# First norm of a two-layer attention trunk: half of the row tiles squared from a second load of x; another matmul price for the planner

## The chip, the cores and the metric

The kernel runs on one core of a Trainium2 chip. The metric is the time of one execution on the device in microseconds (us), as the median of several runs. Profiles show one execution: TensorE (PE, its weight loads PEld), VectorE (DVE), ScalarE (ACT), GpSimd (POOL) and SyncE (SP), which issues all DMAs here.

## The reference

The trunk has two layers, each x <- x + W_out(mixer(RMSNorm(x)) * silu(gate)), with x of 1024 rows by 1024 columns in float32. Layer A is a sliding-window attention (window 128, 16 query heads, 2 key heads, a sink per head). Layer B is a dilated attention with three groups of heads whose results are merged by their softmax denominators. One input projection gives queries, keys, values and the gate. The part that the change touches is the norm ahead of layer A (its mixer gets h = rmsnorm(x, norm_a)):

```python
def rmsnorm(x, g):
    xf = x.astype(jnp.float32)
    y = xf * jax.lax.rsqrt(jnp.mean(xf * xf, axis=-1, keepdims=True) + EPS)
    return (y * g.astype(jnp.float32)).astype(x.dtype)

def mixer_a(h, w_in, q_gain, k_gain, sinks, cos, sin):
    z = h @ w_in
    q, k, v, gate = jnp.split(z, [nq, nq + nk, nq + 2 * nk], axis=-1)
    ...
    return o.reshape(b, s, BRANCH_WIDTH) * jax.nn.silu(gate)
```

## The kernel before

**Tiles and numbers.** The 1024 rows are 8 row tiles of 128 (t = 0 to 7), the 1024 input columns 8 blocks of 128 (k). Each float32 operand of a matmul is split into a rounded high part (fp32r, made by a copy on ScalarE) and a low part (the difference, on VectorE); each product is three matmuls: high with high, high with low, low with high (`mm3`). So a projection of one row tile is 8 x 3 = 24 matmuls (`proj_tile`, tiles `psz`).

**The front.** The input holds x twice: as it is, and as `xt`, in which each row tile is laid out transposed, with the columns of x on the partitions. `load_xt` (tiles `xt`, three buffers, two DMAs for each tile) loads it, `split` makes `hT` from it, the first operand of the projection. The gain of the norm is multiplied into the weights when they are split (`load_w`: loads `raw` or, for half of the first block, `wbig`; splits `wt`). The factor 1 / rms of each row comes in after the matmuls, as the scale with which ScalarE copies the result `psz` out of PSUM into `z`. For that factor, line 761 on, each row tile's x is squared in its transposed layout (`sqx`, on GpSimd since `SQ` is 0), summed over the blocks k by VectorE (`sr`, 128 x 1024 to 128 x 128), transposed by TensorE (`pr`), summed over what is then the free dimension by VectorE (`nss`), and raised to the power -1/2 by GpSimd (`rstd`, into `ra`). `proj_tile` has two PSUM buffers, so the matmuls of tile t + 2 wait until ScalarE has copied out tile t, and so for `ra` of tile t. `z` goes to DRAM and is fetched again for the attention (`bounce`, `fetch`).

**The rest.** Layer A runs four such blocks of heads, with gate blocks (`psg`) and output products (`psw`) between them; layer B twelve (four blocks of heads, three groups each). A unit of attention (128 in all) is: transposes of queries and keys (`pq`), scores (`pss`), a scaled maximum on VectorE, exponentials on ScalarE (`pe`), transposes (`ptt`), the product with the values (`po`), and a merge of heads. Projections and output products are independent of it, and are set between its steps on TensorE. `norm_scale` is the second norm's square, on ScalarE with a running sum (`hn`).

**What sets the order.** Class `Plan` records all instructions in program order and then issues them by a list scheduler. Each instruction has a price in ns (`_cost`), and each pair of engines a latency. At each step the engine that is free first takes, of the instructions whose operands are there, the one with the lowest number, which is its place in program order minus a bias. So the order on every engine, SP included, follows from the prices; on the chip each engine keeps to that order and waits where an operand isn't there. The price of a DMA is its size at 300 bytes per ns, behind the DMAs issued before it, plus fixed times. Buffers of one tag are used in turn (a ring): the instruction that first writes a buffer waits for the last user of its former content.

Of the kernel before, what the change touches and what calls it, by code (L numbers as in the profile page):

```python
# [12 lines left out]
F32 = mybir.dt.float32  # L13
F32R = mybir.dt.float32r
AF = mybir.ActivationFunctionType
OP = mybir.AluOpType
AX = mybir.AxisListType.X

P = 128
D = 1024  # L20
T = 1024
NT = T // P
NK = D // P
# [10 lines left out]
SQ = 0  # L34
# [19 lines left out]
NB = {"pz": 2, "pS": 2, "pT": 2, "pO": 1, "pM": 1}  # L54
# [40 lines left out]


class Plan:
    """Records the instructions in program order, then issues them engine by engine in the order
    that a list scheduler finds: of the instructions whose operands are there, the earliest in
    program order first, so that the projections fill what the attention leaves of TensorE."""  # L100

    ENGINES = ("PE", "ACT", "DVE", "POOL", "SP")
    LAT = {("PE", "PE"): 0, ("PE", "ACT"): 200, ("PE", "DVE"): 200, ("PE", "POOL"): 200, ("PE", "SP"): 200,
# [141 lines left out]
def _cost(eng, name, out, ins):  # L245
    n = out.free_size()
    if eng == "PE":
        if name == "transpose":
            return 109
        return 213 if n < 2 * P else n / 2.4 + 3  # L250
    if eng == "SP":
        return out.size() * 4 / 300.0
    if eng == "DVE":
        if name == "tensor_reduce":
            n = ins[0].free_size()
        if name == "reciprocal":
            return 60 + 6.5 * n
        if name == "tensor_scalar":
            return 130 + 0.53 * n
        return (140 if name in ("tensor_tensor_reduce", "scalar_tensor_tensor") else 70) + 1.04 * n  # L260
    if eng == "ACT":
        return (60 if len(ins) == 1 else 160) + 0.84 * n
    return 150 + 2.1 * n
# [27 lines left out]
def trunk(ctx, tc, x, norm_a, w_in_a, q_gain_a, k_gain_a, sinks_a, w_out_a,  # L291
          norm_b, w_in_b, q_gain_b, k_gain_b, w_out_b, xt, const, out):
    nc = Plan(tc)
    x, out = x[0], out[0]
# [4 lines left out]
    def pool(name, bufs=1, **kw):  # L299
        return ctx.enter_context(tc.tile_pool(name=name, bufs=bufs, **kw))  # L300

    cp = pool("const")
    sp = pool("work")
# [5 lines left out]
    pM = pool("pm", NB["pM"], space=PS)  # L309
# [1 line left out]
    def f(ap):  # L311
        return ap.bitcast(F32)

# [1 line left out]
    ident = nc.tile(cp, [P, P], F32, name="ident")  # L315
    make_identity(tc.nc, ident)
    con = nc.tile(cp, [P, CS_W + 6 * P], F32, name="con")
# [10 lines left out]
    def load_xt(t):  # L328
        a = nc.tile(sp, [P, NK, P], F32, tag="y", bufs=3, name="xt")
        for k in range(0, NK, 4):  # L330
            nc.sync.dma_start(a[:, k:k + 4], xt[t][:, k:k + 4])
        return a
# [35 lines left out]
    x1d = tc.dram_tile([T, D], F32, name="x1d")  # L368
    xpd = tc.dram_tile([T, D], F32, name="xpd")

# [1 line left out]
    def split(hi, lo, src, g=None, sub=nc.vector):  # L372
        if g is None:
            nc.scalar.activation(hi, src, AF.Copy)
            sub.tensor_tensor(lo, src, f(hi), op=OP.subtract)
        else:
            nc.scalar.activation(hi, src, AF.Copy, scale=g)
            nc.vector.scalar_tensor_tensor(lo, src, g, f(hi), op0=OP.mult, op1=OP.subtract)
# [25 lines left out]
    def rstd(dst, ss, mul, add):  # L404
        nc.gpsimd.tensor_scalar(dst, ss, mul, add, op0=OP.mult, op1=OP.add)
        nc.gpsimd.tensor_tensor(dst, dst, ex[:, :dst.shape[1]], op=OP.pow)

    def alloc_h(j):
        return [nc.tile(sp, [P, NK, 2 * P], F32R, tag=f"h{i}{j}", bufs=1, name="hT") for i in range(2)]
# [243 lines left out]
            nc.sync.dma_start(zi[sl, :width], view(zd))  # L653
        return zi

    # ================= layer A =================
    hT = [alloc_h(j) for j in range(4)]
    hB = {}

    def w_a(n, big=None):  # L660
        return load_w(w_in_a, (0, 384, 640, 1024)[n], 256 if n % 2 else 384, 0, big=big)
# [85 lines left out]
    for n in range(4):  # L747
        w = w_a(n, None if n else nc.tile(sp, [P, 4, 512], F32, tag="v0", bufs=1, name="wbig"))
        if n % 2 == 0:
            ak = nc.tile(sp, [P, 2, NT, P], F32R, tag="v0", bufs=1, name="akr")  # L750
            kv = [ak, nc.tile(sp, [P, NT, P], F32R, tag="v2", bufs=1, name="akv")]
        width = 384 if n % 2 == 0 else 256
        if n == 0:
            zd = tc.dram_tile([T, width], F32, name="za0")
            for t in range(NT):
                nc.bias = FRONT if t < FT else 0
                xr = load_xt(t) if t else xt0
                for k in range(0, NK, 4):
                    split(*(a[:, k:k + 4, t % 2 * P:(t % 2 + 1) * P] for a in hT[t // 2]), xr[:, k:k + 4])
                nc.bias = 0  # L760
                sq = nc.tile(sp, [P, NK, P], F32, tag="p", bufs=2, name="sqx")
                if t < SQ:
                    nc.scalar.activation(sq, xr, AF.Square)
                else:
                    nc.gpsimd.tensor_tensor(sq, xr, xr, op=OP.mult)
                sr = nc.tile(sp, [P, P], F32, tag="zi", bufs=3, name="sr")
                nc.vector.tensor_reduce(sr, sq.rearrange("p k t -> p t k"), axis=AX, op=OP.add)
                pr = nc.tile(pM, [P, 4, P], F32, tag="m", bufs=NB["pM"], name="pr")
                nc.tensor.transpose(pr[:, 0], sr, ident)
                ss = nc.tile(sp, [P, 1], F32, tag="nss", bufs=2, name="nss")  # L770
                nc.vector.tensor_reduce(ss, pr[:, 0], axis=AX, op=OP.add)
                rstd(ra[:, t:t + 1], ss, 1.0 / D, EPS)
                if t == LC:
                    late_constants()
                z = proj_tile(hT, t, w, width, ra)
                nc.sync.dma_start(zd[t * P:(t + 1) * P], z[:, :width])
            pr = nc.tile(pM, [P, 4, P], F32, tag="m", bufs=NB["pM"], name="pr")
            nc.tensor.transpose(pr[:NT, 0], ra, ident)
            rr = nc.tile(sp, [NT, P], F32, tag="zi", bufs=3, name="rr")
            nc.vector.tensor_copy(rr, pr[:NT, 0])  # L780
            rd = tc.dram_tile([1, T], F32, name="rd")
            nc.sync.dma_start(rd.rearrange("a (t p) -> (a t) p", p=P), rr)
            rb = [nc.tile(sp, [P, 512], F32, tag="o0", bufs=2, name="rb") for _ in range(2)]
            for i in range(2):
                nc.sync.dma_start(rb[i], rd[:, i * 512:(i + 1) * 512].to_broadcast([P, 512]))
            oa = nc.tile(sp, [P, 4, 2, 2 * P], F32, tag="v1", bufs=1, name="oa")
        else:
            zd = bounce(hT, w, width, f"za{n}", ra)
        wg = load_w(w_in_a, 1280 + n * 256, 256, 0)
        g = gate_block(hT, wg, rb)  # L790
        if n == 3:
            nc.bias = WOA
            y = load_y(0, 0, range(4), sub=YA)
            load_wout_a(range(4), wo, WOA)
            for t in range(6):
                out_a_first(t, None if t else y)
                if t == KA:
                    load_wout_a(range(4, NK), wo, 0)
        for t in range(NT):
            if n == 3 and t in (4, 6):  # L800
                out_a(t - 4)
                out_a(t - 3)
            if t % 2 == 0:
                o = oa[:, t // 2]
                rc = nc.tile(sp, [P, 4, 2], F32, tag="rc", bufs=2, name="rc")
            z = fetch(zd, width, [(slice(0, P), lambda a: a[t * P:(t + 1) * P])])
            qs, r = prep(0, 0, t, z, 5 if n % 2 == 0 else 4, kv if n % 2 == 0 else None, t)
            sk = nsink[:, 4 * n:4 * n + 4]
            nm = nc.tile(sp, [P, 4], F32, tag="nm", bufs=2, name="nm")
            l = nc.tile(sp, [P, 4], F32, tag="l", bufs=2, name="l")  # L810
            slots = [t - 1, t] if t else [0]
            mask = mask_a[:, P:3 * P] if t else mask_a[:, :P]
            tsl = slice(t % 2 * P, (t % 2 + 1) * P)
            attend(qs, r, kv, slots, mask, nm, l, sk,
                   [(o[:HD, :, tsl], slice(0, P))], [(o[HD:, :, tsl], slice(0, P))])
            e = nc.tile(sp, [P, 4], F32, tag="e", bufs=2, name="e")
            nc.vector.tensor_tensor(e, nm, sk, op=OP.subtract)
            nc.scalar.activation(e, e, AF.Exp)
            nc.vector.tensor_tensor(l, l, e, op=OP.add)
            nc.vector.reciprocal(rc[:, :, t % 2], l)  # L820
            if t % 2:
                late.append(partial(merge, 0, n, t // 2, rc[:, None], 1, [o], g))
# [5 lines left out]
    w0 = out_a_whole((6, 7))  # L828
    hT = hB

    # ================= layer B =================
    kk = nc.tile(sp, [P, 2, 4, P], F32R, tag="v2", bufs=1, name="kring")
    kring = [kk, nc.tile(sp, [P, 4, P], F32R, name="vring")]
    ucount = [0]
# [162 lines left out]
```

## Time and profile before

| | |
|---|---|
| time, median of 3 runs | 1298.51 us (1296.77 to 1298.76) |
| span of the profiled execution | 1295.1 us |
| instructions | 25655 |
| moved by DMA | 149.74 MB |

The span runs from the first to the last instruction of one execution and leaves out what lies around it. In the rows further down, an order of time names the start, the length (of several merged instructions together), the engine, the line, the operation, output <- inputs by tile names, sizes, and in brackets the idle time of the engine just before and whom it waited for. As nearly every instruction is recorded by one helper, all have line 286, and tiles tell them apart. The busy time of a matmul includes its way through the array, so that matmuls in a run overlap, and the spacing of a run is shorter than the mean of one.

### The profile page before, as it was taken

The page shows a single profiled execution, that of the slowest core. Times are in us where ns is not written, and L with a number is a line of the kernel's source. Part 1 is how long each engine was busy: PE and PEld are TensorE (multiplying, and loading weights), DVE is VectorE, ACT ScalarE, POOL GpSimd, SP SyncE. Part 2 cuts the span into 40 slices and gives each one's busy share as a digit, 9 for nine tenths or more (in the row PEclk, how much of TensorE's full clock was granted, in tenths as well). Part 3 has the DMA queues.
Part 4 walks back from the last instruction along what each step waited for, and adds up shares of the span by engine and source line. Part 5 has one row for each costly group of instructions (what it writes and reads, how often), then busy time and mean ns, then how long its engine had stood idle before and what let it go on. Part 6 is the DMA issues. An engine that isn't in the chain of part 4 may idle for free. (4 is left out here: it accounts for less than half of the span.)

```text
span 1295.1 us, 25655 instructions
## 1 busy us (share of the span) xinstructions
PE 1257.3 (97%) x7851; PEld 1132.2 (87%) x7851; DVE 1032.6 (80%) x2968; ACT 867.9 (67%) x2365; POOL 703.6 (54%) x1388
## 2 busy tenths in 40 slices
PE   6999999999999999999999999999999999999998
PEld 5999999998778999988889988889988888887777
DVE  8778778777965338778888888988778888779995
ACT  4376766767653347877757877767877767887760
POOL 4764455446410046555577656577556566587621
PEclk9999999999999999999999999999999999999999
DMA  7423223346254133223334323334223344354544
GB/s 242 128 76 110 77 85 102 91 161 185 83 166 142 66 112 100 82 62 105 117 112 128 88 74 94 107 106 137 82 69 106 98 124 133 117 156 135 165 141 157
DMA packets 142666, 149.74 MB, mean 116 GB/s; under 512 B 33576, under 2 KB 129344, under 8 KB 142528
## 3 DMA queue, kind: packets, MB, share of 16 engines
q1 hardware_dynamic: 142528, 148.09, 37.3%
q8 instruction: 63, 1.03, 0.3%
q14 instruction: 75, 0.61, 0.2%
HBM read 105.57 MB, written 42.47 MB: 114 GB/s over the span
## 5 line engine op out<-in xcount | busy, mean ns | idle before, releaser
L286 PE MATMUL psz<-wt,hT 128*128 128x384 f32 (+1 forms) x3072 | 640.9, 344 | 6.1 <-ACT wt L286 3.9
L286 PEld LDWEIGHTS psz<-wt,hT 128*128 128x128 f32 x3072 | 512.9, 191 | 14.8 <-ACT wt L286 4.0
L286 PE MATMUL psg<-hT,wt 128*128 128x256 f32 x1536 | 226.0, 291 | 0.0
L286 ACT ACTIVATE pe<-pe,st 128x128 f32<-128x128 f32 (+1 forms) x384 | 169.5, 443 | 59.8 <-DVE st L286 57.4
L286 PEld LDWEIGHTS psg<-hT,wt 128*128 128x128 f32 x1536 | 203.9, 192 | 2.7
L286 PE MATMUL ptt<-ident,pe 128*128 128x128 f32 x800 | 177.3, 281 | 6.2 <-ACT pe L286 5.4
L286 DVE SCALAR_TENSOR_TENSOR qs<-pq,gt,qs 64x256 fp32r<-64x256 f32 x256 | 123.8, 484 | 42.4 <-ACT qs L286 36.0
L286 POOL TENSOR_TENSOR r<-r,ex 128x5 f32<-128x5 f32 (+1 forms) x128 | 152.8, 1194 | 5.9
L286 ACT ACTIVATE qs<-pq,gt 64x256 fp32r<-64x256 f32 x256 | 120.1, 469 | 46.2 <-PE pq L286 41.0
L286 DVE TENSOR_TENSOR pp<-ptt,pp 128x512 fp32r<-128x512 f32 x200 | 131.7, 685 | 20.9 <-ACT pp L286 18.1
L286 POOL TENSOR_TENSOR sq<-zi 128x320 f32<-128x320 f32 (+1 forms) x128 | 93.4, 730 | 88.0 <-DMA zi<-zb 41.1
L286 PEld LDWEIGHTS ptt<-ident,pe 128*128 128x128 f32 x800 | 104.6, 140 | 39.8 <-ACT pe L286 23.6
L286 DVE CUSTOM_DVE_ANT_0 pe<-pss,con,r 128x256 f32<-128x256 f32 x288 | 127.7, 476 | 10.5 <-PE pss L286 8.7
L286 ACT ACTIVATE oh<-po 64x512 f32<-64x512 f32 x128 | 76.1, 595 | 81.3 <-PE po L286 79.8
L286 DVE SCALAR_TENSOR_TENSOR wt<-raw,gt,wt 128x384 fp32r<-128x384 f32 (+1 forms) x188 | 109.9, 615 | 23.8 <-ACT wt L286 22.6
L286 POOL TENSOR_SCALAR r<-ss 128x5 f32<-128x5 f32 (+1 forms) x128 | 31.1, 243 | 179.3 <-DVE st L286 96.4
L286 ACT ACTIVATE pp<-ptt 128x512 fp32r<-128x512 f32 x200 | 111.5, 594 | 19.2 <-PE ptt L286 18.0
L286 PE MATMUL po<-pp,vring 128*128 128x512 f32 x280 | 107.7, 413 | 2.4 <-DVE pp L286 1.8
L286 PE MATMUL psw<-hT,wy 128*128 128x512 f32 x384 | 105.7, 405 | 0.0
L286 ACT ACTIVATE wt<-raw,gt 128x384 fp32r<-128x384 f32 (+1 forms) x188 | 100.0, 564 | 6.4 <-PE psw L286 2.4
L286 PE MATMUL pss<-kring,qs 128*128 128x256 f32 x560 | 94.3, 285 | 0.8 <-DVE kring L286 0.6
L286 PEld LDWEIGHTS pss<-kring,qs 128*128 128x128 f32 x560 | 84.4, 188 | 9.8 <-DVE kring L286 3.1
(142 smaller groups left out, 2115.6 us busy)
## 6 DMA issues: line engine op xcount, KB each, us to landing
raw<-in_w_in_b_dram SPq DMA_DIRECT2D x96, 192.0 KB
zb<-z SPq DMA_DIRECT2D x96, 192.0 KB
cb<-cd SPq DMA_DIRECT2D x128, 128.0 KB
zi<-zb SPq DMA_DIRECT2D x64, 192.0 KB
raw<-in_w_in_a_dram SPq DMA_DIRECT2D x48, 128.0 KB
yraw<-yd SPq DMA_DIRECT2D x24, 256.0 KB
zi<-zb SPq DMA_DIRECT2D x64, 96.0 KB
xt<-in_xt_dram SPq DMA_DIRECT2D x16, 256.0 KB
```

The lines of the kernel that those rows point to most:

```text
L286: self.plan.add(self.name, method, lambda: fn(*args, **kw), outs, ins, dur, func)
```

## The change

For odd row tiles (t = 1, 3, 5, 7) the row tile of x is loaded a second time, in its natural layout (`xn`, 128 x 1024, 512 KB, rows on the partitions), and ScalarE squares it with the sum over the free dimension as a second output. That is the sum for each row; the GpSimd square, both VectorE reductions and the transpose of these tiles are gone. `xn` takes its buffer from the ring `p` of two, as `sqx` does. The transposed load and the split into `hT` stay. Even tiles are as before. The second edit is in the planner's price of a matmul: n / 2.4 + 3 ns for n of 256 and more columns, 213 ns below, becomes n / 2.4 + 13 ns, at least 108. Comments were taken out too.

```diff
@@ _cost
     if eng == "PE":
         if name == "transpose":
             return 109
-        return 213 if n < 2 * P else n / 2.4 + 3
+        return max(108, n / 2.4 + 13)
@@ the loop over row tiles of the first block
                 nc.bias = 0
-                sq = nc.tile(sp, [P, NK, P], F32, tag="p", bufs=2, name="sqx")
-                if t < SQ:
-                    nc.scalar.activation(sq, xr, AF.Square)
+                if t % 2:
+                    xn = nc.tile(sp, [P, D], F32, tag="p", bufs=2, name="xn")
+                    nc.sync.dma_start(xn, x[t * P:(t + 1) * P])
+                    ss = nc.tile(sp, [P, 1], F32, tag="nss", bufs=2, name="nss")
+                    nc.scalar.activation(xn, xn, AF.Square, accum_out=ss)
                 else:
-                    nc.gpsimd.tensor_tensor(sq, xr, xr, op=OP.mult)
-                sr = nc.tile(sp, [P, P], F32, tag="zi", bufs=3, name="sr")
-                nc.vector.tensor_reduce(sr, sq.rearrange("p k t -> p t k"), axis=AX, op=OP.add)
-                pr = nc.tile(pM, [P, 4, P], F32, tag="m", bufs=NB["pM"], name="pr")
-                nc.tensor.transpose(pr[:, 0], sr, ident)
-                ss = nc.tile(sp, [P, 1], F32, tag="nss", bufs=2, name="nss")
-                nc.vector.tensor_reduce(ss, pr[:, 0], axis=AX, op=OP.add)
+                    sq = nc.tile(sp, [P, NK, P], F32, tag="p", bufs=2, name="sqx")
+                    if t < SQ:
+                        nc.scalar.activation(sq, xr, AF.Square)
+                    else:
+                        nc.gpsimd.tensor_tensor(sq, xr, xr, op=OP.mult)
+                    sr = nc.tile(sp, [P, P], F32, tag="zi", bufs=3, name="sr")
+                    nc.vector.tensor_reduce(sr, sq.rearrange("p k t -> p t k"), axis=AX, op=OP.add)
+                    pr = nc.tile(pM, [P, 4, P], F32, tag="m", bufs=NB["pM"], name="pr")
+                    nc.tensor.transpose(pr[:, 0], sr, ident)
+                    ss = nc.tile(sp, [P, 1], F32, tag="nss", bufs=2, name="nss")
+                    nc.vector.tensor_reduce(ss, pr[:, 0], axis=AX, op=OP.add)
                 rstd(ra[:, t:t + 1], ss, 1.0 / D, EPS)
```

## Rows read from the trace of the kernel before

**Rows 1.** The page: busy time, share and instructions; TensorE's slices in tenths.

```profile
PE 1257.3 (97%) x7851; PEld 1132.2 (87%) x7851; DVE 1032.6 (80%) x2968; ACT 867.9 (67%) x2365; POOL 703.6 (54%) x1388
PE   6999999999999999999999999999999999999998
```

**Rows 2.** Busy time by stage: stretch, length, PE, PEld, DVE, ACT, POOL, clock, DMA, GB/s.

```profile
0.00:50.00 50.00, 38.03 (x182) 33.36 (x183) 41.52 (x49) 19.97 (x36) 26.87 (x32) 1.00 0.58 188
...
10.97:18.20 7.23, 6.16 (x17) 4.92 (x18) 6.45 (x7) 4.21 (x8) 5.05 (x4) 1.00 0.92 314
...
100.00:1250.00 1150.00, 1128.10 (x7088) 1016.94 (x7087) 925.73 (x2748) 805.36 (x2218) 634.76 (x1275) 1.00 0.37 111
```

**Rows 3.** TensorE in order of time, 10 to 54 us, parts of it.

```profile
10.97 4.42 PE L286 MATMUL psz<-wt,hT 128*128 128x384 f32 x12
...
17.96 3.47 PE L286 MATMUL psz<-wt,hT 128*128 128x384 f32 x18 [0.67 <-DVE wt L286]
21.66 0.33 PE L286 MATMUL pr<-ident,sr 128*128 128x128 f32 x1 [0.23 <-DVE sr L286]
...
24.45 4.95 PE L286 MATMUL psz<-wt,hT 128*128 128x384 f32 x27
31.72 0.33 PE L286 MATMUL pr<-ident,sr 128*128 128x128 f32 x1 [2.32 <-DVE sr L286]
31.80 4.09 PE L286 MATMUL psz<-wt,hT 128*128 128x384 f32 x22
...
46.16 0.33 PE L286 MATMUL pr<-ident,sr 128*128 128x128 f32 x1 [0.34 <-DVE sr L286]
...
53.62 2.43 PE L286 MATMUL psg<-hT,wt 128*128 128x256 f32 x19
```

**Rows 4.** Single tiles of the front: count, shortest, median, longest in ns.

```profile
L286 PE MATMUL psz<-wt,hT x192: 331/335/690, 6.5 to 53.4; 128*128 128x384 f32 x192
L286 DVE SCALAR_TENSOR_TENSOR wt<-wbig,gt,wt x4: 610/1430/2246, 12.4 to 15.7; 128x384 fp32r<-128x384 f32 x4
L286 DVE TENSOR_REDUCE sr<-sqx x8: 1868/1966/2007, 8.5 to 44.1; 128x128 f32<-128x1024 f32 x8
L286 SPq DMA_DIRECT2D xt<-in_xt_dram x16: 327/422/1167, 1.2 to 33.5; - x16
L286 ACT ACTIVATE hT<-xt x16: 611/622/632, 3.8 to 40.5; 128x512 fp32r<-128x512 f32 x16
```

**Rows 5.** VectorE in order of time, 12 to 20 us.

```profile
12.43 5.48 DVE L286 SCALAR_TENSOR_TENSOR wt<-wbig,gt,wt 128x384 fp32r<-128x384 f32 x4 [0.78 <-ACT wt L286]
17.83 1.88 DVE L286 TENSOR_TENSOR hT<-xt,hT 128x512 fp32r<-128x512 f32 x3
```

**Rows 6.** GpSimd in order of time, from 13 us.

```profile
13.20 4.29 POOL L286 TENSOR_TENSOR sqx<-xt 128x1024 f32<-128x1024 f32 x2 [0.61 <-DMA xt<-in_xt_dram]
```

**Rows 7.** Who TensorE waited for, 10 to 56 us: total, times, longest.

```profile
PE pr L286 <- DVE sr L286: 3.6, 5, 2.3
```

**Rows 8.** The second norm's squares on ScalarE: count, shortest, median, longest in ns.

```profile
L286 ACT ACTIVATE hn<-part x6: 1044/1062/1067, 373.1 to 424.4; 128x1024 f32<-128x1024 f32 x6
```

**Rows 9.** The last run of output matmuls; one gate matmul alone.

```profile
1263.14 28.25 PE L286 MATMUL psw<-hT,wy 128*128 128x512 f32 x123
...
L286 PE MATMUL psg<-hT,wt x51: 278/283/366, 53.6 to 59.9; 128*128 128x256 f32 x51
```

**Rows 10.** TensorE in order of time: projection matmuls between the steps of one attention unit.

```profile
660.53 1.48 PE L286 MATMUL psz<-wt,hT 128*128 128x384 f32 x7
...
663.76 1.83 PE L286 MATMUL psz<-wt,hT 128*128 128x384 f32 x9
...
668.30 1.13 PE L286 MATMUL psz<-wt,hT 128*128 128x384 f32 x5
```

**Rows 11.** Who TensorE waited for, 100 to 1250 us: the largest two of 14.

```profile
PE ptt L286 <- ACT pe L286: 5.4, 8, 1.5
PE pc L286 <- DVE cg L286: 4.5, 5, 1.4
```

## Prediction

> **What bounds the kernel now.** First the page's busy times and slices [rows 1]: TensorE is busy for 97% of the span, VectorE 80%, ScalarE 67%, GpSimd 54%, and TensorE's digit is below 9 only in the first slice (6) and the last (8). Second the stages [rows 2]: TensorE is idle for 50 - 38.0 = 12.0 us of the first 50, and for only 1150 - 1128.1 = 21.9 us from 100 to 1250, at a granted clock of 1.00. So a change can gain in two places: in the front, where the first projection (192 matmuls, 24 for each of 8 row tiles) starts while x and the weights still arrive, and in the scattered waits of the long middle. The end, from 1263 us, is one run of output matmuls [rows 9] and stays.
>
> Third, TensorE in order of time in the front [rows 3]. The first gate matmul, which follows the first projection, starts at 53.62. From 10.97 on, some 185 projection matmuls were left. In an undisturbed run 27 of them take 4.95 us, and one alone 0.335 [rows 3, 4]: (4.95 - 0.335) / 26 = 0.177 us of spacing. 185 x 0.177 = 32.7 us, with an estimated 0.9 for the transposes between them 33.6; TensorE took 42.65. So 9.0 us are lost there, the most that a change to the first norm can give back. The busy share hides part of it: the 12 matmuls at 10.97 are drawn as 4.42 us of work, where 12 x 0.177 = 2.1 would do.
>
> Fourth, who is late. VectorE's order of time shows two culprits. One is the weights: four splits wt<-wbig from 12.43 take 5.48 us [rows 5], the shortest 0.61 and the longest 2.25 [rows 4]. They lie beside two GpSimd squares of x, 4.29 us from 13.20 [rows 6]. After these end, at 17.49, VectorE's next operations run at 1.88 / 3 = 0.63 us each [rows 5]. So the squares on GpSimd stretch VectorE's work on the weights, and TensorE waits for that: 0.67 us at 17.96 [rows 3], more of it hidden. The other is the chain of the norm, sr - pr - nss: the reduction takes 1.97 us [rows 4], and TensorE, in order, waits with its transpose pr, 3.6 us in all [rows 7]: 0.23 for tile 1 (21.66), 2.32 for tile 3 (31.72), 0.34 for tile 7 (46.16) [rows 3], and 0.7 for the even tiles.
>
> **The change, part by part.** *Weights, 10.97 to 18.3.* The square of tile 1 is the first of the two at 13.20, and it leaves GpSimd. Without it the four splits take 4 x 0.61 = 2.4 us and end near 14.9, and tile 0's last matmul near 15.5. It is 18.3 now: 1 + 6 + 12 + 4 = 23 are through before 17.96, and the 24th is the first of the 18 there. Gain 2.8 us. It holds if tile 2's square, which stays on GpSimd, doesn't just move up. It can't start before its x has landed, now by 13.20 + 4.29 / 2 = 15.35 at the latest, and the new load of xn is ahead of it on SP, by program order: 512 KB at the 314 GB/s of that stretch [rows 2] are 1.7 us. If it moves up all the same, I take half, 1.4.
>
> *The odd tiles' chain.* Four reductions of 1.97 us, four short ones, four transposes and four GpSimd squares go. VectorE loses 4 x 1.97 = 7.9 us and a little, of 41.5 in the first 50 [rows 2]. TensorE loses the waits of the odd tiles, 0.23 + 2.32 + 0.34 = 2.9 (tile 5 has none), and four transposes, each of which sets the next matmul back by 0.08 us (31.72 to 31.80) [rows 3]: 0.3. Of the even tiles' 0.7 I count 0.4, since VectorE gets to them earlier. Sum 3.6.
>
> *What is added.* Four squares with a sum on ScalarE: the same form costs 1.06 us later in this kernel [rows 8], 4.2 in all beside 20.0 busy of the first 50 [rows 2]. That costs nothing, as long as ScalarE doesn't stand at the head of its queue waiting for xn; the scaled copies z and the x splits hT are queued behind it, and TensorE waits for both. SP issues four more DMAs, 0.42 us each [rows 4], and 2.1 MB more pass: 188 GB/s over the first 50 us become 230, against 314 in the fullest stretch [rows 2]. Pushed back are x of tile 2 and, later in SP's order, con and rg, which serve the attention and with it nothing ahead of the gate matmul at 53.62. x of tile 2 would land at 15.35 + 1.7 = 17.05 at the latest; two copies on ScalarE (0.62 each [rows 4]) and a split on VectorE (0.63) make 18.9, and TensorE asks for it at 15.5 + 24 x 0.177 = 19.8. This is the thin place: 0.9 us of cover. Without it 1 to 2 us come back at each even tile. The two buffers that xn shares alternate between xn and the squares, so that xn of tile 3 waits for the square of xn of tile 1, nothing later.
>
> Front: 2.8 + 3.6 = 6.4. I take 6, with 2 (the cover gone) and 9 (all that is lost) as ends.
>
> *The matmul price.* No matmul in the code is narrower than 256 columns (transposes have their own price), so the new floor of 108 ns never acts. The edit adds 10 ns to each: 384 columns 163 to 173 ns, 512 columns 216 to 226, 256 columns 110 to 120. The trace says 177; 28.25 / 123 = 230; and (2.43 - 0.28) / 18 = 119 [rows 3, 9]. All were priced 6 to 8% too low and are now within 2%. No work is added; only the order on every engine is found anew, over the whole program. Two effects oppose each other. A planner with a truer price sets the other engines' queues nearer to the times at which operands really come. But a matmul priced too low is also a reserve: TensorE reaches each step that hangs on another engine later than planned. Between the transpose of kk and the scores of a unit of attention I count 7 fillers, up to the transposes of its exponentials 9, and up to the output product 5 [rows 10]: 21 x 10 ns, 0.2 us per unit, over 128 units 27 us, if each hand-over were just in time. They aren't: from 100 to 1250 us the named waits are 43, 19.4 us together, the two largest groups 5.4 in 8 and 4.5 in 5 [rows 11]. 43 x 0.1 us would be 4 more. I take zero, between -11 (half of the 21.9 go) and +13 (half of the 27 come): nearer to the 4 than to the 27, and with a gain of that size from the truer queues set against it.
>
> So the span becomes 1295.1 - 6 = 1289.1. The median of the runs, 1298.51, is 3.4 us above the span of the profiled execution: 1289.1 + 3.4 = **1292.5 us**.
>
> **The rivals.** *B: the new order closes waits in the middle too.* For it: the largest waits there are for ScalarE and VectorE [rows 11], which were idle for 30 and 19% of that time [rows 2], so order is at fault more than capacity. Against it: there are only 21.9 us to be had. If 8 go: 1284.5. *C: the truer price uses up the reserve.* Place: the hand-overs of the attention units from 100 us on. Price: 0.1 us each, more where a late step delays the next unit. It makes the kernel slower than before once it costs more than the 6 us and the 2.6 that can be told from no change, 86 late hand-overs of some 512 (four per unit). At 12: 1304.5. Against it: most hand-overs show no wait at all now. The Trainium skill, in TensorE: Matmul & The Clock Gate, section Back-to-back issue gap, speaks for C: it calls the formula N/2.4 + 2.5, almost the old price, too high for wide matmuls in a stream, and gives 131 ns for 512 columns. By that the new 226 would be 95 ns too dear and attention steps would be planned far too early; the trace, with 230 ns [rows 9], disagrees. *D: the front's gain doesn't arrive:* xn holds up x of the even tiles, or ScalarE stands behind xn, or an even tile's reduction is set as badly as tile 3's was. 2 us are left: 1296.5. That the edit doesn't do what it says can be excluded for the squares, whose old operations are gone from the code; for the price it is the dead floor.
>
> **How the numbers follow.** Forecast 0.40 (1289 to 1296), B 0.18, C 0.25, D 0.17. A difference under 0.2% (2.6 us, so 1295.9 to 1301.1) can't be told from no change. Faster: 0.39 + 0.18 + 0.03 of D = 0.60. Same: 0.01 + 0.13 of D + 0.03 of C = 0.17. Slower: 0.22 of C + 0.01 of D = 0.23. The range, 1282 to 1306, leaves out the far end of B and of C.
>
> **What would show it.** Right: the splits wt<-wbig near 0.61 us each; no wait of pr for odd tiles; the first gate matmul near 47.6 in place of 53.62; no wait of ScalarE for xn over 1 us; the matmul spacings unchanged at 177, 230 and 119 ns; 19 to 25 us of idle TensorE from 100 to 1250. Wrong: a first gate matmul later than 51, or an idle time of the middle that moves by over 5 us either way.

## The result and the profile after

The changed kernel takes 1333.38 us (median; 1332.35 to 1337.15) against 1298.18 before: a ratio of 1.0274, 95% interval 1.0256 to 1.0292. It is 35 us slower; 1292.5 was forecast. The profiled execution has a span of 1335.3 us (1295.1 before). First the page of after, its busy times and TensorE's slices, beside [rows 1]:

```profile
PE 1282.1 (96%) x7847; PEld 1131.6 (85%) x7847; DVE 1026.1 (77%) x2960; ACT 874.3 (65%) x2373; POOL 697.1 (52%) x1384
PE   7999999999999999999999999989999999999998
```

TensorE has the same work, less four transposes, and is "busy" for 25 us longer, while the other engines' shares fall. No other engine has become the bound. The front did what was forecast. TensorE in order of time, after, beside [rows 3]:

```profile
10.96 10.31 PE L286 MATMUL psz<-wt,hT 128*128 128x384 f32 x50
21.77 0.33 PE L286 MATMUL pr<-ident,sr 128*128 128x128 f32 x1 [0.50 <-DVE sr L286]
21.85 10.99 PE L286 MATMUL psz<-wt,hT 128*128 128x384 f32 x61
33.81 0.33 PE L286 MATMUL pr<-ident,sr 128*128 128x128 f32 x1 [0.97 <-DVE sr L286]
...
48.19 1.24 PE L286 MATMUL psg<-hT,wt 128*128 128x256 f32 x9
```

The first gate matmul starts at 48.19 in place of 53.62. From there on it goes wrong. Three marks divide the rest: the last two squares of the second norm (`hn<-x`, the end of layer A), and the first and the last copy of a gate block in layer B (`gT<-psg`). The rows give count, shortest, median and longest in ns, then first and last start in us; before first, then after:

```profile
L286 ACT ACTIVATE hn<-x x2: 1042/1046/1051, 425.5 to 431.9; 128x1024 f32<-128x1024 f32 x2
L286 ACT ACTIVATE gT<-psg x16: 593/597/602, 510.9 to 1116.2; 128x512 f32<-128x512 f32 x16
```

```profile
L286 ACT ACTIVATE hn<-x x2: 1051/1056/1061, 442.8 to 447.9; 128x1024 f32<-128x1024 f32 x2
L286 ACT ACTIVATE gT<-psg x16: 578/598/601, 528.0 to 1155.6; 128x512 f32<-128x512 f32 x16
```

So 5.4 us are won up to the gate, 17.3 + 5.4 = 22.7 lost between there and 442.8 (layer A), none up to 528.0, 627.6 - 605.3 = 22.3 lost in the long stretch of layer B, none after it (179.7 to the end, 178.9 before). Below, "A" is the start of the first of these squares and "B" the length of the stretch between the gate copies.

How such a loss looks in the rows: busy time from 100 to 1250 us (columns as in [rows 2]) and the largest wait of TensorE there (as in [rows 11]).

```profile
100.00:1250.00 1150.00, 1114.32 (x6899) 987.32 (x6899) 896.56 (x2650) 785.88 (x2163) 622.03 (x1257) 1.00 0.35 107
```

```profile
PE ptt L286 <- ACT pe L286: 7.4, 20, 2.0
```

Idle time grew from 21.9 to 35.7 us only, named waits from 43 (19.4 us) to 76 (31.4 us). The granted clock is 1.00 in both. But 189 fewer matmuls were done in the same 1150 us (6899 for 7088). Most of the loss isn't drawn as idle time, because a matmul is drawn with its way through the array: a transpose for 0.27 to 0.33 us, though the next may follow after 0.11, and a matmul of 384 columns for 0.34, though the next may follow after 0.17. After, TensorE in order of time in layer B:

```profile
699.94 0.33 PE L286 MATMUL ptt<-ident,pe 128*128 128x128 f32 x1
700.29 0.30 PE L286 MATMUL pq<-ident,kk 128*128 128x128 f32 x1
...
705.73 0.27 PE L286 MATMUL ptt<-ident,pe 128*128 128x128 f32 x1
705.76 0.60 PE L286 MATMUL psz<-wt,hT 128*128 128x384 f32 x2
...
711.12 0.38 PE L286 MATMUL pq<-ident,zi 128*128 128x128 f32 x2
711.26 2.35 PE L286 MATMUL psz<-wt,hT 128*128 128x384 f32 x12
```

From 699.94 to 700.29 a transpose keeps the next one waiting for 0.35 us, and no bracket says so; undisturbed it is 0.11 (below). Of 0.35 us, 0.24 are lost unseen.

The same rows show what a transpose costs TensorE, which the case turns on. A matmul starts only 0.03 us after a transpose (705.73 to 705.76), and the usual start of the next transpose is 0.11 us later. But the matmul that starts so early holds up what follows it: the two matmuls at 705.76 are drawn as 0.60 us, so that the second starts 0.60 - 0.335 = 0.265 us after the first, where 0.174 is usual. Over all pairs in the trace of before, the median spacing is 120, 174 and 231 ns from a matmul of 256, 384 and 512 columns to the next instruction, but 202, 259 and 315 ns, some 84 more, where that matmul comes right behind a transpose. So a transpose costs 109 ns when another transpose follows (536 cases) and 28 + 84 = 112 ns when a matmul does (737 cases).

With the counts, 2688 x 174 + 2720 x 120 + 1168 x 231 + 536 x 109 + 737 x 112 ns = 1205 us of work for TensorE, an estimate that holds for both kernels. The planner, who prices every transpose at 109, added up 1128 us before and 1194 after. So the old plan took TensorE to be 6% faster than it is, all of it by the matmuls, and the new plan is within 1%. The truer plan is the slower one. The time that TensorE loses, span less work, is 1295 - 1205 = 90 us before and 131 after.

### The profile page after: what moved, and what is told of

Same layout as the page of the kernel before. It is cut to its first block, busy times and chain, and to the rows that moved or that the text cites. A ratio compares the mean times of both kernels' runs of the same rounds, so it can differ in the third digit from the quotient of the medians.

```text
span 1335.3 us, 25640 instructions
## 1 busy us (share of the span) xinstructions
PE 1282.1 (96%) x7847; PEld 1131.6 (85%) x7847; DVE 1026.1 (77%) x2960; ACT 874.3 (65%) x2373; POOL 697.1 (52%) x1384
## 4 chain that ended last, share of the span: by engine, by line
PE 44%; DVE 29%; ACT 11%; DMA 6%; issue 6%; POOL 3%; SPq 2%; DVEq 0%; ACTq 0%; POOLq 0%
PE psz L286 15%; PE psw L286 8%; DVE pe L286 7%; PE psg L286 6%; DVE og L286 4%; ACT pe L286 4%; PE po L286 4%; PE ptt L286 4%; PE pss L286 3%; DVE wt L286 3%; DVE qs L286 3%; DVE pp L286 3%; DMA cb<-cd 2%; PE pq L286 2%; ACT qs L286 2%
## 5 line engine op out<-in xcount | busy, mean ns | idle before, releaser
L286 PE MATMUL psz<-wt,hT 128*128 128x384 f32 (+1 forms) x3072 | 648.0, 344 | 4.9 <-ACT wt L286 4.2
L286 PE MATMUL ptt<-ident,pe 128*128 128x128 f32 x800 | 181.9, 287 | 10.1 <-ACT pe L286 8.1
L286 PEld LDWEIGHTS ptt<-ident,pe 128*128 128x128 f32 x800 | 101.1, 140 | 55.0 <-ACT pe L286 36.6
L286 ACT ACTIVATE wt<-raw,gt 128x384 fp32r<-128x384 f32 (+1 forms) x188 | 97.2, 563 | 14.7 <-DMA raw<-in_w_in_b_dram 6.7
L286 PE MATMUL psw<-hT,wy 128*128 128x512 f32 x384 | 102.8, 402 | 0.0
```

The costliest lines, as they stand in the source:

```text
L286: self.plan.add(self.name, method, lambda: fn(*args, **kw), outs, ins, dur, func)
```

## The experiments

Two theories stood at the start. The reserve, from the prediction: a matmul priced too low makes TensorE late at each hand-over, and each ns taken away costs. The redraw: the order before is a lucky one and any other is worse, whatever the size of the edit. A third, the balance, came out of the first eight runs: what counts is TensorE's price as a whole against the other engines, for it decides how many projection matmuls ("fillers") are set between two steps of attention. It also held that the old transpose price was too high and made up for the matmul price; the pairs above show that it wasn't. All runs against the kernel before on the same chip; ratio with its 95% interval.

| run | us | ratio | A | B | B's end to the end |
|---|---|---|---|---|---|
| before | 1298 | | 425.5 | 605.3 | 178.9 |
| whole change | 1333.38 | 1.0274 (1.0256 to 1.0292) | 442.8 | 627.6 | 179.7 |
| front only | 1294.58 | 0.9966 (0.9952 to 0.9979) | 423.6 | 604.8 | 179.1 |
| price -7 | 1308.15 | 1.0068 (1.0051 to 1.0085) | 435.2 | 586.8 | 203.8 |
| price -1 | 1313.38 | 1.0115 (1.0094 to 1.0136) | 438.4 | 606.7 | 185.1 |
| price +1 | 1314.67 | 1.0128 (1.0113 to 1.0144) | 435.3 | 609.5 | 182.1 |
| price +5 | 1328.07 | 1.0230 (1.0211 to 1.0250) | 435.6 | 624.1 | 178.6 |
| price +10 (price only) | 1337.41 | 1.0305 (1.0290 to 1.0320) | 443.9 | 629.1 | 180.4 |
| price +20 | 1385.31 | 1.0677 (1.0661 to 1.0693) | 457.7 | 656.8 | 178.8 |
| +10 in layer A only | 1312.49 | 1.0116 (1.0098 to 1.0135) | 443.4 | 604.9 | 179.9 |
| +10 in layer B only | 1325.31 | 1.0213 (1.0198 to 1.0228) | 426.8 | 628.5 | 180.3 |
| +10, later to TensorE | 1337.91 | 1.0313 (1.0296 to 1.0330) | 443.2 | 631.1 | 179.9 |
| +10, transposes 62 | 1317.70 | 1.0151 (1.0129 to 1.0172) | 442.9 | 607.9 | 182.0 |
| transposes 62 only | 1328.79 | 1.0230 (1.0205 to 1.0255) | 443.0 | 600.2 | 203.2 |
| whole change, transposes 62 | 1308.96 | 1.0084 (1.0062 to 1.0107) | 434.2 | 608.1 | 181.4 |
| front, -7 in layer B | 1307.54 | 1.0068 (1.0048 to 1.0089) | 419.9 | 590.1 | 207.1 |
| latency +1 | 1304.62 | 1.0051 (1.0036 to 1.0067) | 425.6 | 607.3 | 183.4 |

**The two edits apart.** The front alone (the change with the old price), and the price alone:

```diff
-        return max(108, n / 2.4 + 13)
+        return 213 if n < 2 * P else n / 2.4 + 3
```

> The first norm is changed (odd tiles squared from a second load), the matmul price stays n/2.4 + 3. The order of TensorE is almost that of the kernel before (214 differing lines out of some 2400 grouped ones). If the loss of the whole change comes from the price alone, the front's gain of 5.4 us (first gate matmul at 48.19 in place of 53.62) is kept to the end: 1292 to 1294 us. If the second load or the new squares disturb the rest, 1300 us or more.

> The first norm is as before, the price is n/2.4 + 13. If the two edits act by themselves, the loss is that of the whole change plus the front's gain: 1333.4 + 5 = 1338 us, with the waits of TensorE for steps of attention units raised by some 35 us over before, hidden ones included. If it takes both edits to lose, 1296 to 1303 us.

Nearly as expected: 1294.58, faster than both kernels, and 1337.41. The front gains 0.34%, the price loses 3.05%, and they add. So the price is the cause of the loss. Of the 4.7 us that the front alone wins up to the first gate matmul (at 48.9), 1.9 are left at mark A.

**Small doses, both ways.** `n / 2.4 + 4` and `n / 2.4 - 4`:

> The first norm is as before, the price is n/2.4 + 4, one ns over before (the floor never acts). TensorE's order differs in 4469 grouped lines, about as much as with ten ns more (4618). Theory of the reserve (a matmul priced low makes TensorE late at each hand-over, and each ns taken away costs): a tenth of the loss, 1300 to 1304 us. Theory of the redraw (any new order is worse than the one that the old price happened to give, whatever the size of the edit): as slow as the whole change, 1315 to 1340 us.

> The first norm is as before, the price is n/2.4 - 4, seven ns under before. Theory of the reserve: more of it, so not slower than before, 1285 to 1300 us, unless work that other engines plan too early takes over. Theory of the redraw: slower like any other order, 1310 to 1340 us.

Neither theory holds alone. One ns costs 1.28% in all, far over a tenth of the loss, but most of it in layer A (10 us, 435.3 for 425.5). Layer B follows the dose: 586.8 at -7, 609.5 at +1, 629.1 at +10. The gate copies at -7 and +10 (price only):

```profile
L286 ACT ACTIVATE gT<-psg x16: 587/598/600, 516.6 to 1103.4; 128x512 f32<-128x512 f32 x16
```

```profile
L286 ACT ACTIVATE gT<-psg x16: 577/598/601, 529.0 to 1158.1; 128x512 f32<-128x512 f32 x16
```

At -7 the price of it comes at the end, 203.8 us in place of 178.9. The end on TensorE, -7 first, then the whole change, beside [rows 9]:

```profile
1277.10 0.37 PE L286 MATMUL pc<-ident,cg 128*24 128x128 f32 x1 [3.12 <-DVE cg L286]
1278.83 8.10 PE L286 MATMUL psw<-hT,wy 128*128 128x512 f32 x24 [1.37 <-ACT wy L286]
1294.84 8.59 PE L286 MATMUL psw<-hT,wy 128*128 128x512 f32 x24 [7.91 <-ACT wy L286]
```

```profile
1292.97 38.60 PE L286 MATMUL psw<-hT,wy 128*128 128x512 f32 x169
```

Before, 123 output matmuls were left over when the last attention step was done. At -7 the fillers are used up too early and TensorE waits for the last operands wy, 7.91 us; with the change 169 are left, 46 more that were not set between earlier steps. The clock adds to the end at -7: the granted clock was 0.69 and 0.64 over the two runs of 24, part of the time at 1.2 in place of 2.4 GHz, with waits of 3.12 and 7.91 us ahead of them, and they took 8.10 and 8.59 us where 24 x 0.23 = 5.5 do at the full clock [rows 9].

**Dose and place.** `n / 2.4 + 23`; ten ns on the matmuls of layer B alone (a shift set at its first loop); later, with the layers the other way round, and `n / 2.4 + 8`:

```diff
+            if method == "matmul":
+                dur += self.plan.shift
...
         for g in (2, 1, 0):
+            nc.shift = 10
```

> The first norm is as before, the price is n/2.4 + 23, twenty ns over before. The measure is the stretch of layer B between its first and its last copy of a gate block, which took 605.3 us before, 586.8 at -7, 609.5 at +1 and 629.1 at +10 ns. Theory of the reserve: it goes on growing by 2 to 2.5 us for each ns, 645 to 655 us, and the whole lies at 1355 to 1380. Theory of the redraw: no slope, about as at +10, 600 to 632 us, and 1310 to 1345 in all.

> The first norm is as before; only the matmuls recorded from layer B on cost ten ns more, those of layer A keep their price. Theory of the reserve: layer A takes its old time (the second norm's last two squares begin near 425.5 us), the stretch between layer B's first and last gate copies grows from 605 to 625 to 632 us, and the whole comes to 1318 to 1326. If the loss is laid in layer A and only handed on, 1296 to 1303.

> The first norm is as before; only the matmuls recorded in layer A cost ten ns more, layer B's keep their price. If the two layers' losses add up (17 to 18 us in A, 23 in B), the second norm's last squares begin at 440 to 446 us (425.5 before), the stretch between layer B's gate copies is 602 to 609, and the whole 1310 to 1320 us.

> The first norm is as before, the price is n/2.4 + 8, half of the change's step. By the slope of the doses so far (586.8 at -7, 605.3 at 0, 629.1 at +10, 656.8 at +20) the stretch between layer B's gate copies is 615 to 620 us; layer A loses 10 to 17 like all other prices, and the whole is 1317 to 1328 us.

B grows to 656.8 at +20, just over what was expected, 70 us over 27 ns of dose, 2.6 us for each ns; the stretch holds some 3100 matmuls, so most of each ns that the planner adds to a matmul shows on the chip, though no matmul takes longer (120, 174 and 231 ns in the trace of after too). At +20 the whole is beyond what was expected, since layer A loses 32 us as well. The layers' losses nearly add: A alone 14.7 us in all with B untouched (604.9), B alone 27.4 with A untouched (426.8), 39.3 together. At +5, B is 624.1, a little over the line that I expected.

**Giving the reserve back by latencies.** Price +10, and 100 ns more from ScalarE, VectorE and GpSimd to TensorE:

```diff
-           ("ACT", "PE"): 285, ("ACT", "ACT"): 200, ("ACT", "DVE"): 155, ("ACT", "POOL"): 65, ("ACT", "SP"): 150,
-           ("DVE", "PE"): 260, ("DVE", "ACT"): 130, ("DVE", "DVE"): 130, ("DVE", "POOL"): 160, ("DVE", "SP"): 150,
+           ("ACT", "PE"): 385, ("ACT", "ACT"): 200, ("ACT", "DVE"): 155, ("ACT", "POOL"): 65, ("ACT", "SP"): 150,
+           ("DVE", "PE"): 360, ("DVE", "ACT"): 130, ("DVE", "DVE"): 130, ("DVE", "POOL"): 160, ("DVE", "SP"): 150,
...
```

> The first norm is as before, the price is n/2.4 + 13, and the planner's latency from ScalarE, VectorE and GpSimd to TensorE is 100 ns longer, so that each hand-over to TensorE gets a reserve by another way (21 fillers of 10 ns are 70 ns for each of three hand-overs of a unit). Theory of the reserve: most of the loss comes back, the stretch between layer B's gate copies is 600 to 612 us, and the whole 1298 to 1315. Theory of the redraw, or of a price that does harm by itself: about as slow as with the price alone, 1325 to 1345.

B stays at 631.1 and the whole at 1337.91: nothing comes back. A longer planned latency doesn't replace a low price; the table at the end of the next part shows what it does instead.

**The balance.** New matmul price and transposes at 62 ns, the mean of 109 and 28 by count (28 is the start of the next matmul alone, so 62 is 47 to 50 ns below the cost); 62 ns with the old matmul price; and the whole change with 62:

```diff
         if name == "transpose":
-            return 109
+            return 62
```

> The first norm is as before, matmuls cost n/2.4 + 13 and a transpose 62 ns in place of 109. In the trace a transpose that is followed by another keeps the next one away for 109 ns, one that is followed by a matmul for 28 only, 536 and some 737 of them: 62 on average. Theory of the balance (what counts is TensorE's price as a whole against the other engines: before, transposes priced 47 ns too high, 60 us in all, stood against matmuls priced 10 ns too low, 66 us; the new matmul price alone makes TensorE look slower than it is): most of the loss comes back, the stretch between layer B's gate copies is 600 to 614 us (629 with the matmul price alone), the whole 1298 to 1315. Theory that the matmul price by itself does it: 622 to 632 and 1325 to 1345.

> The first norm and the matmul price are as before, a transpose costs 62 ns. Theory of the balance: TensorE is now priced 60 us too low, as with nine ns less for each matmul: the stretch between layer B's gate copies falls from 605 to 580 to 592 us, and the end is stretched, since the fillers run out ahead of the attention units: 1300 to 1320 in all. Theory that only the matmul price counts: 602 to 608 us in that stretch.

> The whole change, and a transpose at 62 ns. Theory of the balance: the matmul price's loss mostly gone, the front's gain kept, 1292 to 1310 us. Otherwise 1325 to 1340.

With TensorE's sum brought from 1194 back to 1134 us, B comes back from 629.1 to 607.9, though each matmul keeps its ten ns. So in layer B it isn't the matmul's price by itself that costs, but how long the planner takes TensorE's work to be. Of the balance, this part holds. The other part doesn't: no error was made good, for 1134 us is again 6% less than the 1205 that TensorE needs. Layer B was fast both times with a plan that takes TensorE to be faster than it is, which is what the theory of the reserve says, for the stage as a whole. The gate copies with +10 and 62:

```profile
L286 ACT ACTIVATE gT<-psg x16: 590/599/602, 526.2 to 1134.1; 128x512 f32<-128x512 f32 x16
```

The whole, 1317.70, is above the 1298 to 1315 expected, because layer A doesn't come back (442.9). The whole change gets 24 us of its 35 back (1308.96), as expected; it stays slower than the kernel before. With transposes alone cheaper (sum 1068) the whole, 1328.79, is over the 1300 to 1320 expected, and B, 600.2, fell by 5 us only, for 13 to 25 expected. Here B's mark misleads. The gate matmuls of that run:

```profile
L286 PE MATMUL psg<-hT,wt x1536: 274/283/369, 54.5 to 1101.5; 128*128 128x256 f32 x192
```

They are through at 1101.5, 578 us after the first gate copy (523.4), for 604 before (510.9 to 1115.3): 26 us less, as the planned sum lets expect. With them the fillers were used up, and the last gate copy came 22 us later. From 1100 to 1124 TensorE was busy for 14 of 24 us, waiting for steps of attention, at a granted clock of 0.58.

Where the time goes in layer B can be worked out from the traces: for each instruction of TensorE between the first and the last gate copy, the spacing from the one before, less the usual spacing above. Sums in us by what came late, in brackets the cases over 30 ns (`pc` is of the merge of heads; fillers are `psz` and `psg`):

| run | ptt | pq | po | pc | pss | fillers | sum |
|---|---|---|---|---|---|---|---|
| before | 13.6 (84) | 9.4 (46) | 7.1 (37) | 4.9 (5) | 3.0 (22) | 6.4 (75) | 44.4 |
| whole change | 23.2 (161) | 14.1 (63) | 7.3 (46) | 5.4 (7) | 5.8 (39) | 8.9 (109) | 64.8 |
| +10 | 23.9 (156) | 13.7 (61) | 8.3 (49) | 5.5 (8) | 6.1 (40) | 8.7 (108) | 66.2 |
| +10, later to TensorE | 19.9 (115) | 13.9 (58) | 12.9 (60) | 8.9 (8) | 2.1 (21) | 8.8 (96) | 66.6 |
| +10, transposes 62 | 16.6 (84) | 7.2 (35) | 5.9 (34) | 7.0 (7) | 4.0 (24) | 6.6 (73) | 47.1 |

So most of layer B's loss is TensorE kept waiting for steps of attention units, nearly twice as often for the transposes `ptt` of the exponentials, and mostly hidden in drawn lengths; and it goes when TensorE is priced low again. The longer latency shortened the waits of `ptt` and `pss` and lengthened those of `po` and `pc`: it moved the waits on. Why a plan with true prices of TensorE serves the steps later than one that is 6% off was not found. The prices of the other engines give no hint: ScalarE's copy of 128x512 is priced 490 ns and is followed after 493, VectorE's difference of 128x512 602 and 601. The latencies were not held against the trace.

**A better kernel?** The front and, in layer B up to its last group, seven ns less (`nc.shift = 0 if n == 3 and g == 0 else -7`):

> The change of the first norm with the old price, and seven ns less for the matmuls recorded in layer B up to the last group of its last block of heads, where the output products come in; those keep the old price. Theory of the reserve: the stretch between layer B's gate copies falls from 605 to 584 to 592 us and the end is not stretched as it was with seven ns less everywhere; 1294.6 - 15 = 1275 to 1284 us, faster than both kernels. Theory of the redraw: a new order in layer B, 1300 to 1320.

A miss. B falls to 590.1, but the time from there to the end grows by 28 us. Keeping the last group's price doesn't help: TensorE waits 9.3 us for wy, as at -7, at a granted clock of 0.96 from the last gate copy on. The gain in B was borrowed from the end, as fillers that are then missing. The front alone, at 1294.58, stays the fastest of all.

**Layer A.** One ns the other way, and one ns on a latency, which is no price of TensorE:

> The first norm is as before, the price is n/2.4 + 2, one ns less than before. In layer A every other price so far (-7, +1, +10, +20) began the second norm's last squares at 435 us or later, the old one at 425.5. If the order that the old price gave in layer A is a single good draw, it is 432 to 440 here too, and the whole 1303 to 1315 although layer B's stretch is 601 to 606; if +1 ns was the odd one, 424 to 428 and 1294 to 1300.

> The first norm and all prices are as before; only the planner's latency from TensorE to ScalarE is 201 ns in place of 200, which means nothing to the chip. If the order of layer A before is a good draw that any edit loses, the second norm's last squares begin at 432 us or later and the whole is 1303 to 1315 us; if it takes a change of the matmul price, 424 to 428 and 1295 to 1301. The stretch between layer B's gate copies stays at 602 to 610 in both.

At -1, A is at 438.4: each matmul price but the old one costs 10 to 32 us there, -1 and +1 alike. The latency leaves A where it was (425.6; 1304.62 in all, a few us lost in layer B and at the end), although some 2600 grouped lines of TensorE's order differ. So it is not that any edit of the planner loses A. But an edit that means nothing to the chip costs 0.5% in all, more than the front's gain at the end of the program. Where I compared the stretches (+1, -1, the whole change), a part of the loss lies about the output products of layer A. Busy time of 300 to 350 us, before and after:

```profile
300.00:350.00 50.00, 47.73 (x254) 38.09 (x252) 43.60 (x115) 38.27 (x94) 33.02 (x52) 1.00 0.42 132
```

```profile
300.00:350.00 50.00, 44.11 (x250) 35.63 (x248) 41.34 (x109) 35.51 (x88) 33.92 (x52) 0.97 0.47 146
```

TensorE idles there for 5.9 us in place of 2.3. The granted clock of 0.97 after isn't the cause: at +1 it is 1.00 there and layer A loses as well. Which instruction's place makes the step of 10 us, and what the rest of layer A's loss is, stays open.

## Why the prediction was wrong

**The front: right, a little too large.** The four splits wt<-wbig take 612 to 619 ns each now, the waits of pr for odd tiles are gone, the first gate matmul is at 48.19 (47.6 forecast). VectorE's splits, after, beside [rows 4]:

```profile
L286 DVE SCALAR_TENSOR_TENSOR wt<-wbig,gt,wt x4: 612/614/619, 12.3 to 13.9; 128x384 fp32r<-128x384 f32 x4
```

So the stretching of VectorE's splits came from GpSimd's square beside them: with it gone they take their shortest time. The Trainium skill, SBUF — State Buffer, section Who interferes with whom, says that a VectorE instruction with two SBUF inputs contends with a GpSimd instruction that reads SBUF, and that a tensor_reduce never does; the trace agrees on both (the split has two such inputs; sr ran 1.87 to 2.01 us [rows 4], 1.93 with no GpSimd square beside it at 8.46 and 1.95 with one at 41.38). The even tiles' reductions still keep pr waiting, 0.50 + 0.97 + 0.33 = 1.8 us where I left 0.3, and ScalarE waited 1.6 us for xn of tile 5, over the 1 us allowed. A transpose `pr` that is gone was worth some 0.17 us, not 0.08: the matmul behind it also holds up the next, by 0.08 more. At the end of the program the front is worth 0.34%, 4.4 us, for 6 forecast.

**The matmul price: the step that failed.** The term was put at zero, as 4 us of late hand-overs against a gain of that size from "a truer price". Neither holds. The price did become true, as the prediction read from its rows (120, 174 and 231 ns for 119.7, 173 and 226.3), and so did TensorE's planned sum, 1194 of 1205 us; but the truer plan gained nothing and lost 3.05%. And the 4 us came from the sentence "They aren't" just in time, drawn from the 43 named waits. Named waits show only what exceeds the drawn length of a matmul. In layer B alone the trace of before has 269 spacings that are over the usual by more than 30 ns, and 44 us over the usual in all; the change made that 65 us, with 161 late transposes `ptt` in place of 84. The 27 us that the prediction gave for hand-overs that are all just in time were far nearer than the 4 that it took: ten ns on layer B alone cost 27.4.

**Its bounds failed with it.** First, -11 and +13 came from the 21.9 us of idle time and from half of those 27. The idle time is the wrong measure: the prediction itself had seen that busy time hides waits in the front, and then took it at face value in the middle. Span less work is 90 us before, and the loss raised it to 131. Second, rival C had the sign, the place and the kind of the loss (late steps of attention units), at a third of the size; that a longer planned latency gives nothing back shows that the reserve isn't one of each hand-over by itself. Third, by taking zero I assumed that a new order is by itself worth as much as the old: the 10 us that layer A loses at -1 and +1 ns alike had no term in the sum. That the old price gave layer A a good order looks like luck; no run shows another reason.

## What to carry to other kernels

A truer price need not make a better plan. Here a list scheduler that took TensorE to be 6% faster than it is gave the better order in the longest stage, by matmuls or by transposes priced too low, so a price is a setting to be tried in both directions, stage by stage, with an eye on the fillers that are left for the end. Measure what an operation costs over the pair: by the start of what follows it, and by how much later than usual the one after that starts. And bound what a new order can lose by span less work, not by drawn idle time; where an edit redraws an order, put a term for that in the sum.

## What the runs showed of the hardware

A float32 transpose of 128 columns keeps the next transpose away for 109 ns. A matmul starts 28 ns after it, but is then followed 82 to 85 ns later than usual (202, 259 and 315 ns for 256, 384 and 512 columns), so that the transpose costs 110 to 113 ns there. Matmuls in a stream are 120, 174 and 231 ns apart for 256, 384 and 512 columns (medians; n / 2.4 + 13 gives 120, 173 and 226), with their weight loads beside them. A split of 128x384 on VectorE takes 0.61 us alone and up to 2.25 us beside a GpSimd square of 128x1024 [rows 4, 6].
